# State-space set-up from turned tables: layouts, the W and T tables, and the order of the GLU's weight rows

## The chip, the cores and the metric

The kernel runs on one core of a Trainium2 chip. The metric is device time in microseconds (us) of one execution; the median of a few runs is compared. TensorE (PE in the profile) multiplies matrices, PEld is its weight load; VectorE (DVE), ScalarE (ACT) and GpSimd (POOL) do elementwise work; SyncE (SP) issues most DMAs, GpSimd's queue some.

## The reference

One inference step of a decoder with two layers, D_MODEL 1024, on a prompt of 512 tokens and 8 samples of 8 tokens: 576 tokens in all. Layer 0 mixes tokens by dilated attention, layer 1 by a diagonal complex state-space layer; each is followed by a gated ffn (D_FF 2816). The change concerns the state-space layer alone:

```python
def ssm_layer(h, state0, w_in, a_re, a_im, log_dt, b_re, b_im, c_re, c_im, d_skip, w_glu):
    u = h @ w_in                                     # 64 groups of 16 channels
    lam = complex(a_re, a_im); dt = exp(log_dt)[:, None]
    abar = exp(lam * dt)                             # (64 groups, 64 states)
    bbar = ((abar - 1) / lam)[..., None] * bmat      # (64, 64, 16)
    # x[t] = abar * x[t-1] + bbar u[t];   y[t] = Re(cmat x[t]) + d_skip * u[t]
    z = gelu(y) @ w_glu
    val, gate = split(z, 2)
    return val * sigmoid(gate), h_last
```

## The kernel before, in words

Activations lie with channels on the 128 partitions and the 576 tokens along the free dimension. A product in fp32 is made of three matmuls on halves hi and lo of both operands (`mm6`, L108). A weight tile of 512 KB is fetched into `raw` (4 buffers, SyncE's queue), ScalarE makes `whi` (L99), VectorE `wlo` (L100), and 48 matmuls use them: about 6.4 us.

In time the core goes through attention (0 to 400 us), the output projection `wo_phase` (to about 423), the ffn of layer 0 (`ffn`, to about 875), the state-space layer (`ssm_phase`, to about 1075) and the second ffn (`ffn_last`). Inside `ffn`, `tick()` is called behind each weight tile and takes one step of the generator `ssm_setup`. That generator makes the tables of the state-space layer while the ffn runs. A scheduler orders each engine's instructions from the program and its dependences; `issue_after` holds an instruction behind another one. SyncE's queue also carries copies of the attention caches (`o_kv_s`), of 1 MB each, a few per weight tile (`pace`).

The tables. Time is cut into 72 columns of 8 steps: an input tile U has 16 channels x 8 steps on the partitions and 72 columns per group. For each of eight blocks f (8 groups each) the set-up makes and writes to DRAM:

- W (`w_scr`): what 8 steps of input add to the state, B times powers of abar;
- V (`v_scr`): what a state gives to 8 steps of output, C times powers of abar;
- T (`t_scr`): the direct part of input on output within 8 steps, a block Toeplitz matrix of the kernel K, with D on its diagonal;
- E (`e_scr`): factors for the scan over columns, for all f at once.

Before: A, dt, C and the state are loaded as they lie and transposed on TensorE (L1386, L1440, L1453). Per f, `powers(f)` makes B times powers on VectorE (`wr`, L1329 to L1334); TensorE transposes it in 8 pieces (L1531) and ScalarE evicts it as W. K is 16 matmuls of `cb` (C in blocks) by `wr` (L1540), copied, transposed once more (L1548), spread by 8 stream shuffles (L1557), and multiplied by a mask (`tmask`, L1562) into T. GpSimd makes V. Two buffers `cb` are cleared at the start of the loop (L1506).

In `ssm_phase`, `stage1` makes u = W_in x, writes it to DRAM (`u_scr`, L1632) and reads it back with 8 steps on the partitions as `U` (L1636). `stage2` makes the states from U and W (L1646), a scan on VectorE follows; `stage3` makes y from U with T and from the states with V (L1687), gelu on ScalarE (L1689), and goes through DRAM again (`y_scr`, L1690, L1692) to the GLU. W, E, T and V of f = 4 to 7 are loaded on GpSimd's queue when buffers come free (L1293 to L1303).

Of the kernel before, what the change touches and what calls it, by code (L numbers as in the profile page):

```python
# [8 lines left out]
F32 = mybir.dt.float32  # L9
# [41 lines left out]
def _build(nc, tc, A, es):  # L51
# [108 lines left out]
    def acc(i=None):  # L160
        if i is None:
# [6 lines left out]
           "T": scr.tile([8, 128, 8, 128], F32, name="t_scr"), "E": scr.tile([8, 128, 2, 4, 64], F32, name="e_scr"), "U": scr.tile([8, 128, NT], F32, name="u_scr"),  # L168
# [1107 lines left out]
def ssm_setup(nc, tc, A, L, keep, out):  # L1276
    v, s, g, te = nc.vector, nc.scalar, nc.gpsimd, nc.tensor
    ident, pool, aux, scn = L["ident"], L["pool"], L["aux"], L["scn"]
    GP = 4096
# [18 lines left out]
    def consts_out(f, q):  # L1298
        kc = kp[f // 2 % 2]
        Tc = kc.tile([128, 8, 128], F32, name="Tc")  # L1300
        q.dma_start(Tc, scn["T"][f])
# [7 lines left out]

    out.update(Ar=Ar, Ai=Ai, E63=E63, rho=rho, x0=x0, xs0=xs0, KC=KC, consts_in=consts_in, consts_out=consts_out)  # L1310
    with ExitStack() as es:
        ct = es.enter_context(pool("ssa"))
        tmask = ct.tile([128, 8], F32, name="tmask")
        with tc.issue_after(L["xload"].ins):
            nc.sync.dma_start(tmask, A["c_tm"])
        dcol = ct.tile([128, KT], F32, name="dcol")
        with tc.issue_after(L["xload"].ins):
            nc.sync.dma_start(dcol, dram(A["ssm_d"], 0, [[1, 128], [128, KT]]))
        U8 = ct.tile([128, 2, 7, 32], F32, name="U8")
        dmask = ct.tile([128, 16], F32, name="dmask")  # L1320
        with tc.issue_after(L["xload"].ins):
            nc.sync.dma_start(dmask, A["c_dm"])
        Br = ct.tile([128, 32, 16], F32, name="Br")
        Bi = ct.tile([128, 32, 16], F32, name="Bi")
        Cr = ct.tile([128, 32, 16], F32, name="Cr")
        Cn = ct.tile([128, 32, 16], F32, name="Cn")
# [9 lines left out]
        with ExitStack() as e2:  # L1336
# [25 lines left out]
            raw = wk.tile([32, 3, 128], F32, name="raw")  # L1362
            with tc.issue_after(L["xload"].ins):
                nc.sync.dma_start(raw[:, 0], dram(A["ssm_a_re"], 0, [[128, 32], [1, 128]]))
            with tc.issue_after(L["xload"].ins):
                nc.sync.dma_start(raw[:, 1], dram(A["ssm_a_im"], 0, [[128, 32], [1, 128]]))
            ldt = wk.tile([32, 2], F32, name="ldt")
            with tc.issue_after(L["xload"].ins):
                nc.sync.dma_start(ldt, dram(A["ssm_log_dt"], 0, [[2, 32], [1, 2]]))
            with tc.issue_after(L["womark"].ins):  # L1370
                v.tensor_copy(raw[:, 2].rearrange("p (a b) -> p a b", a=2), ldt[:, :, None].to_broadcast([32, 2, 64]))
            cw = wk.tile([128, 2, 8, 64], F32, name="cw")
            with tc.issue_after(L["xload"].ins):
                nc.sync.dma_start(cw[:, 0], dram(A["ssm_c_re"], 0, [[64, 128], [8192, 8], [1, 64]]))
            with tc.issue_after(L["xload"].ins):
                nc.sync.dma_start(cw[:, 1], dram(A["ssm_c_im"], 0, [[64, 128], [8192, 8], [1, 64]]))
            bw = wk.tile([128, 2, 32, 16], F32, name="bw")
            with tc.issue_after(L["xload"].ins):
                nc.sync.dma_start(bw[:, 0], dram(A["ssm_b_re"], 0, [[16, 128], [2048, 32], [1, 16]]))
            with tc.issue_after(L["xload"].ins):  # L1380
                nc.sync.dma_start(bw[:, 1], dram(A["ssm_b_im"], 0, [[16, 128], [2048, 32], [1, 16]]))
            yield
            yield
            ps = aux.tile([128, 2, 512], F32, name="aux")
            for i in range(3):
                te.transpose(ps[:, 0, i * 32:(i + 1) * 32], raw[:, i], ident[:32, :32])  # L1386
            pc = wk.tile([128, 3, 32], F32, name="pc")
            v.tensor_copy(pc, ps[:, 0, :96].rearrange("p (a b) -> p a b", a=3))
# [14 lines left out]
            vexp(fl(mag), fl(lr), fl(n[:, :4]), fl(z[:, :4]), fl(sn[:, :4]), fl(ie))  # L1403
            th, n, z, sn, cn = (fl(x) for x in (th, n, z, sn, cn))
# [6 lines left out]
            v.scalar_tensor_tensor(sn, sn, 1.0, th, op0=OP.add, op1=OP.mult)  # L1411
            horner(cn, z, [(-1.0) ** k / math.factorial(2 * k) for k in range(8, 0, -1)])
# [4 lines left out]
            v.tensor_scalar(z, z, -2.0, 1.0, op0=OP.mult, op1=OP.add)  # L1417
            ui, ur = (x.rearrange("p (a b) -> p a b", b=32) for x in (th, z))
# [5 lines left out]
            t1, t2 = wk.tile([128, 4, 32], F32, name="t1"), wk.tile([128, 4, 32], F32, name="t2")  # L1424
            for m, n_ in ((2, 1), (4, 3)):
                w = slice(m + 1, m + 1 + n_)
                bc = lambda x: x[:, m:m + 1].to_broadcast([128, n_, 32])
                cmul(v, Ar[:, w], Ai[:, w], Ar[:, 1:1 + n_], Ai[:, 1:1 + n_], bc(Ar), bc(Ai), t1[:, :n_], t2[:, :n_])
# [3 lines left out]
            yield  # L1432
            yield
            for i, dst in ((0, Cr), (1, Cn)):
                ps = aux.tile([128, 2, 512], F32, name="aux")
                for f in range(8):
                    cwd = wk.tile([128, 2, 64], F32, name="cwd")
                    with tc.issue_after(L["womark"].ins):
                        v.tensor_copy(cwd, cw[:, i, f][:, None, :].to_broadcast([128, 2, 64]))
                    te.transpose(ps[:, f // 4, (f % 4) * 128:(f % 4 + 1) * 128], cwd.rearrange("p a b -> p (a b)"), ident)  # L1440
                for gl in range(2):
                    hs = slice(gl * 64, gl * 64 + 64)
                    for hf in range(2):
                        v.tensor_scalar(dst[hs, hf * 16:hf * 16 + 16, :], ps[hs, hf, :].rearrange("p (q l c) -> p q l c", l=2, c=16)[:, :, gl, :], 1.0 if i == 0 else -1.0, None, op0=OP.mult)
                yield
                yield
            yield
            xw = wk.tile([128, 2, 128, 2], F32, name="cw")
            nc.sync.dma_start(xw, dram(A["state_ssm"], 0, [[256, 128], [32768, 2], [1, 256]]))
            for hf in range(2):  # L1450
                for ri in range(2):
                    ps = aux.tile([128, 2, 512], F32, name="aux")
                    te.transpose(ps[:, 0, :128], xw[:, hf, :, ri], ident)  # L1453
                    v.tensor_copy(x0[:, ri, hf * 4:hf * 4 + 4, :], ps[:, 0, :128].rearrange("p (b q) -> p b q", b=4))
            for ri in range(2):
                for gl in range(2):
                    g.tensor_copy(xs0[ri * 64:ri * 64 + 64, gl], x0[gl * 64:gl * 64 + 64, ri])
# [17 lines left out]
            b12 = wk.tile([128, 2, 32, 16], F32, name="cw")  # L1475
            b1, b2 = b12[:, 0], b12[:, 1]
            bc = lambda x: x[:, :, None].to_broadcast([128, 32, 16])
            cmul(v, Br, Bi, bw[:, 0], bw[:, 1], bc(fr), bc(fi), b1, b2)
            yield
            yield  # L1480
# [21 lines left out]
        with ExitStack() as e2:  # L1502
            wk = e2.enter_context(pool("ssd", bufs=1))
            cb = [wk.tile([128, 4, 2, 16], F32, name=f"cb{i}") for i in range(2)]
            for t in cb:
                v.memset(t, 0.0)  # L1506
            sh = [128, 4, 16, 8]
            wr = {}

            def powers(f):  # L1510
                qs = slice(f * 4, f * 4 + 4)
                bw_ = lambda x: x[:, qs, :, None].to_broadcast(sh)
                rv = lambda x: x[:, 0:8, qs][:, ::-1, :].rearrange("p m q -> p q m")[:, :, None, :].to_broadcast(sh)
                wr[f] = wk.tile([128, 2, 4, 16, 8], F32, name="wr")
                wt = wk.tile([128, 2, 4, 16, 8], F32, name="wt")
                cmul(v, wr[f][:, 0], wr[f][:, 1], bw_(Br), bw_(Bi), rv(Ar), rv(Ai), wt[:, 0], wt[:, 1])
                for i, c in ((0, Cr), (1, Cn)):
                    for gl in range(2):
                        hs = slice(gl * 64, gl * 64 + 64)
                        v.tensor_copy(cb[i][hs, :, gl, :], c[hs, qs, :])  # L1520

            powers(0)
            yield
            yield
            for f in range(8):
                qs = slice(f * 4, f * 4 + 4)
                ps = aux.tile([128, 2, 512], F32, name="aux")
                with tc.issue_after(L["pem"][0].ins):
                    for ri in range(2):
                        for q in range(4):  # L1530
                            te.transpose(ps[:, ri, q * 128:(q + 1) * 128], wr[f][:, ri, q].rearrange("p c s -> p (c s)"), ident)  # L1531
                wo = wk.tile([128, 2, 4, 128], F32, name="wo")
# [354 lines left out]
```

## Time and profile before

| what | value |
|---|---|
| median of 3 runs | 1469.41 us (1469.1 to 1472.06) |
| profiled execution, its own time | 1472.93 us |
| its span | 1471.1 us |
| TensorE busy | 1432.1 us, 97% |
| VectorE, ScalarE, GpSimd busy | 1000.9, 596.0, 334.6 us |
| mean granted TensorE clock | 0.994 |
| moved by DMA | 345.73 MB |

The page gives busy time by engine and by group of instructions (line of the kernel, engine, operation, output <- inputs, count, busy us, mean ns, idle time before it and what ended it). The views of waits list for each engine which event it stood idle for; the timelines list single instructions with their start and length, idle time before them in brackets. In a window's row come its length, then busy us of each engine with the count of instructions, the granted clock, the DMA share and GB/s.

### The profile page before, as it was taken

How to read it: one execution, taken by the hardware profiler on the slowest of the kernel's cores; microseconds unless marked ns; L12 is line 12 of the kernel's file. 1: busy time of each engine (PE TensorE's matmuls, PEld its weight loads, DVE VectorE, ACT ScalarE, POOL GpSimd, SP SyncE). 2: the span in 40 equal slices, each digit the busy share in tenths (PEclk: the TensorE clock that was granted, in tenths of full speed). 3: DMA queues.
4: the chain of work that ended last, by engine and by line, in shares of the span. 5: the costliest groups of instructions: out<-in, count | busy, mean ns of one | idle time of the engine just before them, and what ended most of it. 6: DMA issues, size and time to landing. Idle time of an engine off the chain costs nothing. (4 is left out here: it accounts for less than half of the span.)

```text
span 1471.1 us, 30038 instructions
## 1 busy us (share of the span) xinstructions
PE 1432.1 (97%) x12398; PEld 1341.1 (91%) x12398; DVE 1000.9 (68%) x1696; ACT 596.0 (41%) x962; POOL 334.6 (23%) x410
## 2 busy tenths in 40 slices
PE   9999999999999999999999999699999999999998
PEld 7888777777899999999999999699999999999998
DVE  5898989745578653687777567856587646755772
ACT  4534455465462221223123363434365324532541
POOL 2022131320031066156245330131010001100110
PEclk9999999999999999999999999899999999999999
DMA  7566798999897757888979857964267767775532
GB/s 243 207 232 234 224 306 278 347 307 330 301 298 257 264 216 270 300 298 313 318 269 319 290 178 227 275 181 130 86 169 190 242 216 184 184 244 156 146 110 63
DMA packets 181048, 345.73 MB, mean 235 GB/s; under 512 B 40720, under 2 KB 116304, under 8 KB 179504
## 3 DMA queue, kind: packets, MB, share of 16 engines
q1 hardware_dynamic: 168176, 309.00, 61.4%
q0 software_dynamic: 9968, 32.12, 9.8%
q10 hardware_dynamic: 2768, 2.70, 0.6%
q8 instruction: 97, 1.59, 0.4%
q14 instruction: 39, 0.32, 0.1%
HBM read 312.29 MB, written 118.78 MB: 293 GB/s over the span
## 5 line engine op out<-in xcount | busy, mean ns | idle before, releaser
L108 PE MATMUL acc<-xgh,wlo 128*128 128x288 f32 x1056 | 227.6, 297 | 3.4 <-DVE wlo L100 3.4
L108 PE MATMUL acc<-xgh,whi 128*128 128x288 f32 x1056 | 229.5, 299 | 0.0
L108 PE MATMUL acc<-xgl,whi 128*128 128x288 f32 x1056 | 227.3, 297 | 0.0
L99 ACT ACTIVATE whi<-raw 128x1024 fp32r<-128x1024 f32 x98 | 102.0, 1041 | 242.8 <-PE acc L108 193.9
L1171 PE MATMUL bank<-xoh,whi 128*128 128x288 f32 x616 | 182.5, 296 | 4.2 <-ACT cq L1182 2.8
L1171 PE MATMUL bank<-xoh,wlo 128*128 128x288 f32 x616 | 181.7, 295 | 0.2 <-DVE wlo L1113 0.2
L1171 PE MATMUL bank<-xol,whi 128*128 128x288 f32 x616 | 181.7, 295 | 0.0
L108 PEld LDWEIGHTS acc<-xgh,wlo 128*128 128x128 f32 x1056 | 170.6, 189 | 4.0 <-DVE wlo L100 3.9
L108 PEld LDWEIGHTS acc<-xgh,whi 128*128 128x128 f32 x1056 | 170.3, 189 | 1.8 <-issue 1.2
L108 PEld LDWEIGHTS acc<-xgl,whi 128*128 128x128 f32 x1056 | 170.5, 189 | 0.1
L100 DVE TENSOR_TENSOR wlo<-raw,whi 128x1024 fp32r<-128x1024 f32 x98 | 124.7, 1272 | 67.3 <-ACT whi L99 66.3
L1171 PEld LDWEIGHTS bank<-xoh,whi 128*128 128x128 f32 x616 | 115.7, 188 | 6.1 <-ACT cq L1182 4.4
L1113 DVE TENSOR_TENSOR wlo<-raw,whi 128x1024 fp32r<-128x1024 f32 (+1 forms) x57 | 70.7, 1241 | 73.3 <-ACT whi L1112 73.3
L384 PE MATMUL acc<-whi,xh 128*128 128x512 f32 x288 | 118.7, 414 | 1.6 <-ACT xh L324 1.5
L1171 PEld LDWEIGHTS bank<-xoh,wlo 128*128 128x128 f32 x616 | 115.8, 188 | 0.6 <-DVE wlo L1113 0.6
L1171 PEld LDWEIGHTS bank<-xol,whi 128*128 128x128 f32 x616 | 115.7, 188 | 0.1
L1112 ACT ACTIVATE whi<-raw 128x1024 fp32r<-128x1024 f32 (+1 forms) x57 | 58.4, 1029 | 136.6 <-DMA raw<-ffn_w_down 52.1
L384 PE MATMUL acc<-wlo,xh 128*128 128x512 f32 x288 | 112.2, 391 | 0.0
L384 PE MATMUL acc<-whi,xl 128*128 128x512 f32 x288 | 111.5, 393 | 0.0
L108 PE MATMUL acc<-hh,whi 128*128 128x288 f32 x352 | 76.2, 297 | 0.0
L1080 POOL TENSOR_TENSOR gt<-gt,rstd 128x576 f32<-128x576 f32 x22 | 39.4, 1794 | 160.5 <-ACT gt L1079 160.4
L1127 POOL DMA_DIRECT2D s<-w_gu x22 | 19.4, 883 | 247.3 <-DMA s<-w_gu 145.5
(445 smaller groups left out, 3142.5 us busy)
## 6 DMA issues: line engine op xcount, KB each, us to landing
o_kv_s<-cache_kv_w SPq DMA_DIRECT2D x64, 1020.0 KB, 7.7
kc<-cache_kv_w SPq DMA_DIRECT2D x100, 512.0 KB, 6.9
raw<-ffn_w_down SPq DMA_DIRECT2D x40, 512.0 KB, 3.8
raw<-w_qkv SPq DMA_DIRECT2D x36, 512.0 KB, 7.0
raw<-w_gu SPq DMA_DIRECT2D x33, 512.0 KB, 3.4
kc<-qscr SPq DMA_DIRECT2D x32, 512.0 KB, 6.1
o_kv_s<-cache_kv_w SPq DMA_DIRECT2D x16, 1008.0 KB, 7.5
raw<-ffn_w_gate SPq DMA_DIRECT2D x22, 512.0 KB, 5.1
```

Source lines behind the costliest of these rows:

```text
L99: s.activation(hi, raw, AF.Copy)
L100: mark[0] = v.tensor_tensor(lo, raw, hi.bitcast(F32), OP.subtract)
L108: pem[0] = te.matmul(ps[:, c, :HN], w, x[:, c * HN:(c + 1) * HN], start=first and i == 0, stop=last and i == 2)
L384: ins = nc.tensor.matmul(*a, **kw)
L1080: g.tensor_tensor(t, t, nin.r, OP.mult)
L1112: s.activation(hi, raw, AF.Copy)
L1113: v.tensor_tensor(lo, raw, hi.bitcast(F32), OP.subtract)
L1127: g.dma_start(fl(t), block(c, m, k), accum_op=OP.add)
L1171: tc.keep_in_program_order(te.matmul(acc[q][:, :HN], a[:, k, i * 128:(i + 1) * 128], nin.x[x, k][b], skip_group_check=n != "a12", start=n ...
```

## The change

All small inputs of the state-space layer are laid out on the host as the core wants them (`_ssm`: A and dt, B in two layouts, C, the state, D), and each is loaded without a transpose. The rows of `ssm_w_glu` are reordered to channel within step of the output tile. In the set-up, A times the factor of B is made for all f at once (`af`), transposed by 4 matmuls and written to DRAM (`a_scr`); per f it is read back with its rows repeated 16 times, B with its rows repeated 8 times (`bt`), and VectorE's products of the two are W with channels on the partitions. K is now 16 matmuls of B (`Bz`) by table V (`vx`, 9 powers, made on GpSimd); it is copied into `kk`, 15 blocks of which 7 are zero, and one DMA writes T's 8 overlapping views of it. u is stored with time reversed; y is written in whole rows and read back in pieces of 72 columns. The chain that makes the exponentials no longer waits for a mark behind `wo_phase`, and takes more steps of the generator.

```diff
-    cb = [wk.tile([128, 4, 2, 16], F32, name=f"cb{i}") for i in range(2)]
-    for t in cb:
-        v.memset(t, 0.0)
...
+            def load(f):
+                a = wk.tile([128, 2, 4, 128], F32, name="af")
+                nc.sync.dma_start(a..., dram(scn["A"], f * 8192, [[0, 16], [1024, 8], [1, 1024]]))
+                b = wk.tile([128, 2, 4, 128], F32, name="bt")
+                nc.sync.dma_start(b..., dram(A["s_bt"], f * 16384, [[1024, 16], [0, 8], [1, 1024]]))
+                c = wk.tile([128, 2, 4, 16], F32, name="C", bufs=2)
+                nc.sync.dma_start(c, A["s_c"][:, :, f * 4:f * 4 + 4])
...
-                            te.transpose(ps[:, ri, q * 128:(q + 1) * 128], wr[f][:, ri, q]..., ident)
-                s.activation(wo.rearrange("p r q c -> p r (q c)"), ps, AF.Copy)
-                nc.sync.dma_start(scn["W"][f], wo)
+                for h in range(2):
+                    v.tensor_tensor(t, x, b2(1), OP.mult)
+                    v.tensor_tensor(x, x, b2(0), OP.mult)
+                    v.tensor_tensor(x[:, 0], x[:, 0], t[:, 1], OP.subtract)
+                    v.tensor_tensor(x[:, 1], x[:, 1], t[:, 0], OP.add)
+                    if h:
+                        nc.sync.dma_start(scn["W"][f], a)
...
-                            te.matmul(pk[q * 32:q * 32 + 32, 0, :128], cb[i][:, q]..., wr[f][:, i, q]..., ...)
-                v.tensor_copy(kk, pk[:, 0, :128])
-                    te.transpose(pk[:, 1, :128], kk, ident)
-                    v.stream_shuffle(st[:, t], kt, m)
-                v.tensor_tensor(tt..., st, tmask[:, :, None].to_broadcast([128, 8, 128]), OP.mult)
-                nc.sync.dma_start(scn["T"][f], tt.rearrange("p g c t -> p g (c t)"))
+                            te.matmul(pk[q * 32:q * 32 + 32, 0, :128], Bz[:, i, f * 4 + q]..., vx[:, i, q, 0:8]..., ...)
+                v.scalar_tensor_tensor(k[:, 7], dmask, dcol[:, f:f + 1], pk[:, 0, :16], op0=OP.mult, op1=OP.add)
+                v.tensor_copy(k[:, 8:15], pk[:, 0, 16:128].rearrange("p (t c) -> p t c", c=16))
+                nc.sync.dma_start(scn["T"][f].rearrange("g (c s) x -> (g c) s x", s=8), bass.AP(tensor=k0.tensor, offset=k0.offset, ap=[list(k0.ap[0]), [16, 8], [1, 128]]))
...
-        q.dma_start(Tc, scn["T"][f])
+        q.dma_start(Tc, scn["T"][f].rearrange("g p c -> p g c"))
...
-            v.tensor_tensor(u, ps[m][:, :, :HN], nin.r, OP.mult)
+            v.tensor_tensor(pos(u)[:, ::-1, ::-1, :], pos(ps[m][:, :, :HN]), pos(nin.r), OP.mult)
...
-        nc.sync.dma_start(dram(scn["Y"], f * 128 * NT, [[72, 128], [9216, 8], [1, 72]]), ys...)
+        nc.sync.dma_start(scn["Y"][f], ys.rearrange("p q l c -> p (q l c)"))
-        nc.sync.dma_start(yt, scn["Y"][f])
+        nc.sync.dma_start(yt, dram(scn["Y"], f * 128 * NT, [[72, 128], [9216, 8], [1, 72]]))
```

Three places in the order of instructions. First VectorE at the first norm of the ffn (`rs_m`, `sq`, `rstd`) and its first use (`gt`), before:

```order
L1371 COPY raw<-ldt 32x128
L1439 COPY cwd<-cw 128x128
L100 TENSOR_TENSOR wlo<-raw,whi 128x1024
L181 SCALAR_TENSOR_TENSOR xgl<-xT,gm,xgh 128x576
L100 TENSOR_TENSOR wlo<-raw,whi 128x1024
L212 TENSOR_SCALAR rs_m<-aux 128x288 x2
L214 TENSOR_TENSOR sq<-rstd 128x576
L215 TENSOR_TENSOR sq<-sq,rs_m 128x576
L221 SCALAR_TENSOR_TENSOR rstd<-sq,rstd 128x576
L1078 TENSOR_TENSOR gt<-acc_5403,rstd 128x576
```

and after, where the chain of the exponentials (`z`, `th`, `n`, `mag`) stands among them:

```order
L212 TENSOR_SCALAR rs_m<-aux 128x288
L1386 SCALAR_TENSOR_TENSOR th<-n,th 128x320
L1340 SCALAR_TENSOR_TENSOR z<-z,sn 128x128
L1387 TENSOR_SCALAR th<-th 128x320
L214 TENSOR_TENSOR sq<-rstd 128x576
L1353 TENSOR_SCALAR z<-z 128x128
L215 TENSOR_TENSOR sq<-sq,rs_m 128x576
L1355 TENSOR_TENSOR mag<-z,ie 128x128
L221 SCALAR_TENSOR_TENSOR rstd<-sq,rstd 128x576
L1388 TENSOR_TENSOR z<-th 128x320
L1411 COPY rho<-mag 128x32
L1078 TENSOR_TENSOR gt<-acc_5404,rstd 128x576
```

The chain, which stood behind this norm, now stands ahead of it and between its steps. Second, VectorE at the start of the loop over f, before:

```order
L1506 MEMSET cb_7279 128x128
L1506 MEMSET cb_7280 128x128
L1329 TENSOR_TENSOR wt<-Br,Ar 128x512
L1330 TENSOR_TENSOR wt<-Bi,Ai 128x512
L1520 COPY cb_7279<-Cr 64x4x16 x2
L1520 COPY cb_7280<-Cn 64x4x16 x2
L1331 TENSOR_TENSOR wr<-wt 128x512
L1332 TENSOR_TENSOR wt<-Br,Ai 128x512
L1333 TENSOR_TENSOR wt<-Bi,Ar 128x512
L1334 TENSOR_TENSOR wr<-wt 128x512
L100 TENSOR_TENSOR wlo<-raw,whi 128x1024
```

and the products of W that open it now, from `af` (A's powers, repeated) and `bt` (B, repeated):

```order
L1513 TENSOR_TENSOR wt<-af,bt 128x512
L1514 TENSOR_TENSOR af<-af,bt 128x2x256
L1515 TENSOR_TENSOR af<-af,wt 128x256
L1516 TENSOR_TENSOR af<-af,wt 128x256
L1513 TENSOR_TENSOR wt<-af,bt 128x512
L1514 TENSOR_TENSOR af<-af,bt 128x2x256
L1515 TENSOR_TENSOR af<-af,wt 128x256
L1516 TENSOR_TENSOR af<-af,wt 128x256
L100 TENSOR_TENSOR wlo<-raw,whi 128x1024
```

The clearing of `cb` and the powers are gone from VectorE; products of what two DMAs loaded stand first. Third, SyncE in the state-space layer, where u of the last two blocks (f = 6, 7) goes out and comes back, before:

```order
L87 DMA raw<-ssm_w_glu 128x4x256 x2
L1690 DMA y_scr<-ys 128x8x72
L1632 DMA u_scr<-yt 128x576
L1692 DMA U<-y_scr 128x576
L1632 DMA u_scr<-yt 128x576
L87 DMA raw<-ssm_w_glu 128x4x256
L1636 DMA U<-u_scr 128x8x72
L1690 DMA y_scr<-ys 128x8x72
```

and after:

```order
L87 DMA raw<-ssm_w_glu 128x4x256 x2
L1649 DMA y_scr<-ys 128x576
L1651 DMA U<-y_scr 128x8x72
L1591 DMA u_scr<-yt 128x576 x2
L87 DMA raw<-ssm_w_glu 128x4x256
L1595 DMA U<-u_scr 128x8x72
L1649 DMA y_scr<-ys 128x576
```

The read of y(0), which waits for the write of y(0), moved ahead of both writes of u; these now follow each other.

More of the change, by code (lines that the diff above doesn't have):

```diff
@@ L1360, in vexp @@
                 v.tensor_tensor(y, q, ie.bitcast(F32), OP.mult)
[L1362 to L1376, printed above, removed]
-            bw = wk.tile([128, 2, 32, 16], F32, name="bw")
[L1378 to L1381, printed above, removed]
+            pc = wk.tile([128, 3, 32], F32, name="pc")
+            early(pc, A["s_a"])
+            bw = wk.tile([128, 2, 32, 16], F32, name="bw")
+            early(bw, A["s_b"])
+            early(x0, A["s_x"])
+            for ri in range(2):
+                early(xs0[ri * 64:ri * 64 + 64], dram(A["s_x"], ri * 256, [[512, 64], [64 * 512, 2], [1, 256]]))
+            g.memset(Bz, 0.0)
             yield
             yield
[L1384 to L1388, printed above, removed]
             ar, ai = pc[:, 0], pc[:, 1]
@@ L1427, in ssm_setup @@
                 bc = lambda x: x[:, m:m + 1].to_broadcast([128, n_, 32])
-                cmul(v, Ar[:, w], Ai[:, w], Ar[:, 1:1 + n_], Ai[:, 1:1 + n_], bc(Ar), bc(Ai), t1[:, :n_], t2[:, :n_])
+                f1, f2 = (two[:, i, :n_ * 32].rearrange("p (m q) -> p m q", q=32) for i in range(2))
+                cmul(v, Ar[:, w], Ai[:, w], Ar[:, 1:1 + n_], Ai[:, 1:1 + n_], bc(Ar), bc(Ai), f1, f2)
             v.tensor_copy(rho, mag[:, 3])
@@ L1431, in ssm_setup @@
             v.tensor_copy(U8[:, 1], ui[:, 3:10])
[L1432 to L1457, printed above, removed]
             yield
@@ L1579, in ssm_setup @@
+            yield
         consts(0, nc.sync)
```

154 lines of the change are left out of this document (80 added, 74 removed).

## The prediction

> **What bounds the kernel now.** I read the page's busy times first, then TensorE's waits, then its groups of the set-up, then the timelines at the places where those rows lie.
>
> ```profile
> PE 1432.1 (97%) x12398; PEld 1341.1 (91%) x12398; DVE 1000.9 (68%) x1696; ACT 596.0 (41%) x962; POOL 334.6 (23%) x410
> ```
>
> ```profile
> PE acc L1646 <- DMA U<-u_scr: 11.6, 2, 10.9
> PE acc L108 <- DVE wlo L100: 3.4, 2, 2.5
> ```
>
> TensorE is busy for 1432.1 of 1471.1 us. So an edit pays in two ways only: it takes matmuls out of TensorE's stream, or it shortens one of the few waits. The two largest waits both lie in code that the change touches: 10.9 us in the state-space stage (L1646) and 2.5 us behind VectorE in the ffn (L108). VectorE and ScalarE work saved elsewhere is worth nothing by itself.
>
> **Part 1: transposes leave TensorE.** The set-up runs as a filler between the ffn's weight tiles of 48 matmuls. Its TensorE groups, and ScalarE's start on successive weight tiles (first a stretch without set-up matmuls, then one whole turn of the loop over f):
>
> ```profile
> L1531 PE MATMUL aux<-ident,wr 128*128 128x128 f32 x64 | 8.3, 272 | 0.0
> L1540 PE MATMUL aux<-wr,cb 128*32 128x128 f32 x128 | 5.2, 279 | 0.0
> L1440 PE MATMUL aux<-ident,cwd 128*128 128x128 f32 x16 | 4.3, 271 | 0.0
> L1548 PE MATMUL aux<-ident,kk 128*128 128x128 f32 x8 | 2.2, 271 | 0.0
> ```
>
> ```profile
> 540.95 1.06 ACT L99 ACTIVATE whi<-raw 128x1024 fp32r<-128x1024 f32 x1 [5.29 <-PE acc L108]
> 547.35 1.06 ACT L99 ACTIVATE whi<-raw 128x1024 fp32r<-128x1024 f32 x1 [5.34 <-PE acc L108]
> ...
> 643.55 1.06 ACT L99 ACTIVATE whi<-raw 128x1024 fp32r<-128x1024 f32 x1 [4.13 <-issue]
> 650.72 1.05 ACT L99 ACTIVATE whi<-raw 128x1024 fp32r<-128x1024 f32 x1
> 657.22 1.06 ACT L99 ACTIVATE whi<-raw 128x1024 fp32r<-128x1024 f32 x1 [1.70 <-PE acc L108]
> 663.62 1.06 ACT L99 ACTIVATE whi<-raw 128x1024 fp32r<-128x1024 f32 x1 [1.18 <-DMA o_kv_s<-cache_kv_w]
> 670.88 1.06 ACT L99 ACTIVATE whi<-raw 128x1024 fp32r<-128x1024 f32 x1 [1.90 <-PE acc L108]
> ```
>
> The 271 ns of one transpose is its length in the pipeline, not its price. The price is what a tile takes above 6.40 us (547.35 − 540.95). The four tiles of one f take 7.17, 6.50, 6.40 and 7.26 us. The first holds the 16 kernel matmuls (L1540, +0.77), which stay. The second holds the kk transpose (L1548, +0.10) and the fourth the 8 W transposes (L1531, +0.86): 0.96 us per f, 7.7 us over 8. The 16 C transposes (L1440) and, by the diff, 4 of the state and 3 of A and dt are 23 more at the same 0.11 us: 2.5 us. Four new transposes of af cost 0.4. Net −9.8 us, and this is on the path, since TensorE has no idle time there. The kernel matmuls only exchange their operands, in the same shape: 0.
>
> **Part 2: the wait at the loop's start goes.** SyncE writes e_scr; VectorE's first memset of the loop reuses its memory and waits for the write, and the powers then stand ahead of the next weight split (L100), on which TensorE waits:
>
> ```profile
> 576.83 0.69 SPq L1499 DMA_DIRECT2D e_scr<-ee  x1
> 586.52 0.31 DVE L1506 MEMSET cb<- 128x128 f32 x2 [4.85 <-DMA e_scr<-ee]
> 594.07 1.22 DVE L100 TENSOR_TENSOR wlo<-raw,whi 128x1024 fp32r<-128x1024 f32 x1
> 595.35 0.53 PE L108 MATMUL acc<-xgh,wlo 128*128 128x288 f32 x2 [2.45 <-DVE wlo L100]
> ```
>
> ```profile
> 579.35 1.06 ACT L99 ACTIVATE whi<-raw 128x1024 fp32r<-128x1024 f32 x1 [5.34 <-PE acc L108]
> ...
> 608.98 1.06 ACT L99 ACTIVATE whi<-raw 128x1024 fp32r<-128x1024 f32 x1 [1.36 <-PE acc L108]
> ...
> 597.00:599.00 2.00, 2.00 (x10) 2.00 (x9) 1.59 (x3) 0.98 (x2) 0.21 (x1) 0.50 1.93 760
> ```
>
> These four tiles took 29.63 us instead of 25.60: 4.0 lost, 2.45 waiting and the rest at the granted clock of 0.50 that followed. After the change no VectorE instruction stands there on e_scr: the loads of af and GpSimd's memset of kk do. VectorE first needs af two tiles after its load is issued, 12.8 us against the 9.7 us (576.83 to 586.52) that the write took. So −4.0, with 0 as the other bound.
>
> The Trainium skill ("TensorE: Matmul & The Clock Gate", Part 1) has the half clock follow an idle window of about 3.4 us. Here a wait of 2.45 us was enough (0.50 above); by the page this stall would have cost 2.45 and not 4.0, and the sum would end 1.6 us higher; the trace decides.
>
> **Part 3: the loop over f.** VectorE loses the powers, 8 stream shuffles, the mask multiply and two copies out of PSUM per f, and gains eight products over 256 columns. All that lies beside TensorE, and VectorE is busy for 170.68 of 230 us as it is, so 0; ScalarE loses an eviction, 0; GpSimd's V table grows from 6 operations to 7, and nobody waits for it closely, 0. What grows is DMA: per f, af and bt 512 KB each and C 64 KB, 8.9 MB in all.
>
> ```profile
> 600.00:830.00 230.00, 230.00 (x1826) 227.08 (x1825) 170.68 (x311) 60.84 (x69) 105.65 (x61) 1.00 0.85 298
> ...
> raw<-ffn_w_gate SPq DMA_DIRECT2D x22, 512.0 KB, 5.1
> ```
>
> The DMA engines are 0.85 busy at 298 GB/s, that is 350 GB/s when busy; 8.9 MB is 25.4 us of the 34.5 us (15% of 230) that are idle. Covered, but nearly used up. The cover is the weight prefetch: four raw buffers are about 25 us ahead at 6.4 us a tile, while a tile lands in 5.1. I take +0.5 for small waits; the ends are 0 and +6 (rival C).
>
> **Part 4: VectorE at the start of the ffn.** The set-up's scalar chain no longer waits for a mark behind the w_o stage or for TensorE, so it enters VectorE's queue between the residual adds and the ffn's first norm.
>
> ```profile
> 400.00:425.00 25.00, 25.00 (x190) 25.00 (x189) 21.61 (x42) 13.81 (x20) 9.38 (x6) 1.00 0.99 275
> 425.00:450.00 25.00, 25.00 (x186) 24.58 (x185) 13.97 (x33) 11.72 (x15) 5.62 (x3) 1.00 0.99 353
> ...
> 429.58 1.13 PE L206 MATMUL aux<-ssum,ones 128*128 128x288 f32 x4
> 438.17 1.42 DVE L1078 TENSOR_TENSOR gt<-acc,rstd 128x576 f32<-128x576 f32 x2
> ...
> L1345 DVE SCALAR_TENSOR_TENSOR z<-z,sn 128x32 f32<-128x32 f32 x7 | 1.3, 190 | 0.2
> L1345 DVE SCALAR_TENSOR_TENSOR z<-z,sn 128x128 f32<-128x128 f32 x7 | 3.2, 461 | 0.0
> L1407 DVE SCALAR_TENSOR_TENSOR th<-n,th 128x320 f32<-128x320 f32 x3 | 1.4, 483 | 0.0
> ```
>
> About 13 us of small operations (some 35 of 32 columns at 0.17 to 0.19 us, a dozen of 128 columns, and half a dozen of 320, these rows the dear ones) fall where VectorE idles 3.4 and 11.0 us in the two windows. Much of that idle time is made of waits inside the residual and norm chains, so small operations will delay these. I estimate the last residual 4 us later, the norm's matmuls (L206) stalled about 1.5 us, and gt about 1.5 us too late for TensorE's next accumulator, of which part is the same delay: +2, between 0 and +6 (6 with a half-clock stretch as in part 2).
>
> **Part 5: the state-space stage.** The change writes u reversed and reads y back in another form, and lays T out so that one f's T is read in 1024 runs of 512 B, not 128 rows of 4 KB. SyncE's and GpSimd's queues around the 10.9 us wait, that wait, a window over it, and the landing times of the U reads (L1636) and of the y reads (L1692):
>
> ```profile
> 926.95 0.34 SPq L1632 DMA_DIRECT2D u_scr<-yt  x1
> 930.74 0.33 SPq L1692 DMA_DIRECT2D U<-y_scr  x1
> 931.19 1.27 SPq L1632 DMA_DIRECT2D u_scr<-yt  x1
> 932.50 0.44 SPq L87 DMA_DIRECT2D raw<-ssm_w_glu  x1
> 933.36 0.39 SPq L1636 DMA_DIRECT2D U<-u_scr  x1
> ...
> 929.38 0.53 POOL L1301 DMA_DIRECT2D Tc<-t_scr  x1 [2.29 <-PE acc L1687]
> ...
> 946.14 1.11 PE L1646 MATMUL acc<-U,Wc 128*64 128x72 f32 x14 [10.91 <-DMA U<-u_scr]
> ...
> 938.00:950.00 12.00, 3.86 (x64) 3.89 (x66) 6.97 (x14) 2.40 (x8) 0.00 (x0) 0.50 1.03 302
> ...
> DMA to landing us min/median/max: 3.1/4.6/12.6
> ...
> DMA to landing us min/median/max: 2.7/2.9/5.5
> ```
>
> The read U(6) is issued at 933.36 and lands after 12.6 us, where 4.6 is the median. GpSimd's three pairs of Tc and Vc (3 MB from 929.38 on) fill the engines: 12 us at 302 GB/s is 3.6 MB. SyncE's queue holds then, on each of 16 engines, about 96 small pieces (32 of 1 KB of w_glu, 64 of 288 B of U), GpSimd's 48 of 4 KB. If an engine takes one piece from either queue in turn, SyncE's 96 pieces outlast GpSimd's 48, and everything lands together: 243 KB per engine at 22 GB/s is 11 us, which fits 12.6. With T in 512 B pieces, 96 turns take 64 of 512 B, 8 of 4 KB and 24 of 512 B beside them: 127 KB, 5.8 us. The order also moves: U<-y_scr(0) now stands ahead of u_scr(6), which costs that write 0.5 to 1 us, while the second u_scr, the weight tile and U(6) follow about 2 us earlier. The bounds are −13 (the whole wait and the 2.2 us of half clock behind it) and +4 (the read of y, which waits for a write, blocks the queue). I take −6, an estimate nearer the first mechanism, as short pieces have some cost of their own. At the stage's end the y read in 288 B pieces adds 0.4 us (U reads, in such pieces, take 3.1 us at best; y reads, in rows so far, 2.7).
>
> The Trainium skill ("DMA: Bandwidth & Descriptors", Queues, rings and completion order) has an engine drain a whole packet, some 9 to 17 pieces, from a queue before it switches. By it the size of T's pieces would not decide, and the sum would keep most of the wait (rival A).
>
> **Sum.** −9.8 − 4.0 + 0.5 + 2.0 − 6.0 + 0.4 = −16.9 against the profiled execution's own 1472.93, that is 1456.0. The median of the runs, 1469.41, lies 3.5 below that execution, so 1452.5; I say 1453.
>
> **Rivals.**
> A. The U(6) wait stays, as the same bytes lie in the engines: −10.9, 1459. For it: the DMA share of 1.03 in that window. Against: U moves ahead in its queue. Chance 0.22.
> B. The wait grows by 4, the y read blocking SyncE ahead of u_scr(6): 1463. For it: that read was issued 3.8 us after the instruction ahead of it (926.95 to 930.74). Chance 0.10.
> C. Slower: DMA becomes the bound in the loop. The new loads and the short T pieces would have to cost over twice the 25.4 us that their bytes say: 34.5 are idle, and weights are about 19 us ahead (25 less a landing). From 53.5 us on TensorE starves; the gain is eaten up at 70 us (2.75 times), and at three times (76 us) 23 us are lost and the kernel ends at 1476. For it: the 0.85 share with many short pieces. Chance 0.05.
> D. Part 4's chain costs 6 or more, with half clock, and e_scr's wait only moves to the af loads (+4): 1461. Chance 0.13.
> My forecast, within about 5 us of 1453, has the remaining 0.50.
>
> **How the numbers follow.** The range 1443 to 1463 reaches from the whole U wait gone (−7 more) with a small part 4 (−2) to rivals A and D; about 0.2 is left out, B's upper half and C with it. A measurement here tells about 0.2%, 2.9 us, from no change: faster means below 1466.5. All of the forecast, of A and of D lie below, and 0.04 of B: 0.89. The rest of B, with a larger part 4, and C's milder half are within: 0.07. Slower is the rest of C: 0.04.
>
> **What would show it.** Tiles in the loop of 6.4 us but for one of 7.2 per f; no 0.50 window at 597; a VectorE wait at L206 or L1078 of 1 to 3 us; U(6) landing in 6 to 8 us and a TensorE wait on L1646 of 3 to 6 us; a DMA share near 0.95 in the loop with no weight wait above 1 us. I am wrong if TensorE's waits on raw, af or bt appear in the loop, or if the wait on L1646 stays above 10 us.

## The result: slower by about 0.8%, and the profile after

The changed kernel takes 1481.15 us (median of 5, 1480.14 to 1485.73) against 1470.94 (median of 5, 1469.1 to 1472.65; three of them are the runs behind the 1469.41 above) for the kernel before: a ratio of 1.0076, 95% interval 1.0057 to 1.0095, some 11 us slower. The profiled execution is the longest of the five, 1485.73 us with a span of 1483.9, 4.6 above the median; sums over its trace have to be read with that in mind.

Busy time and TensorE's waits of the changed kernel (line numbers have moved: L1605 is the U product that was L1646):

```profile
PE 1428.0 (96%) x12307; PEld 1335.4 (90%) x12307; DVE 958.2 (65%) x1512; ACT 588.8 (40%) x955; POOL 338.9 (23%) x416
...
PE acc L108 <- DVE wlo L100: 16.9, 6, 11.7
PE acc L1605 <- DMA U<-u_scr: 12.7, 1, 12.7
...
PE aux L206 <- POOL ssum L199: 1.3, 1, 1.3
```

TensorE has 91 matmuls fewer, the number that the prediction counted (95 transposes gone, 4 new), and VectorE is busy for 43 us less. But TensorE's wait behind VectorE, 3.4 us before, is 16.9, and its wait for U, which was to halve, grew from 11.6 to 12.7 in total, the longest from 10.9 to 12.7.

Where the time went is read from ScalarE's starts on weight tiles (L99), the clock of the whole stretch. The two profiled executions differ by 12.8 us in span. Of this, −2.5 lie ahead of the w_o stage and +2.1 behind the stretch around the wait for U, 2.0 of them behind the layer's last weight tile; the code there is the same, so I count both as differences between executions. The rest: +6.4 from the w_o stage to the 22nd tile; +4.0 in the set-up's loop; +0.1 up to the second half of the state-space stage; +2.7 there, in the stretch around the wait for U. The +4.0 is a large loss and two gains. The loss is one place:

```profile
570.41 1.06 ACT L99 ACTIVATE whi<-raw 128x1024 fp32r<-128x1024 f32 x1 [5.34 <-PE acc L108]
591.34 1.06 ACT L99 ACTIVATE whi<-raw 128x1024 fp32r<-128x1024 f32 x1 [19.87 <-PE acc L108]
...
657.36 1.06 ACT L99 ACTIVATE whi<-raw 128x1024 fp32r<-128x1024 f32 x1 [4.49 <-PE acc L108]
664.50 1.06 ACT L99 ACTIVATE whi<-raw 128x1024 fp32r<-128x1024 f32 x1 [1.43 <-PE acc L108]
670.90 1.06 ACT L99 ACTIVATE whi<-raw 128x1024 fp32r<-128x1024 f32 x1 [4.63 <-PE acc L108]
677.30 1.06 ACT L99 ACTIVATE whi<-raw 128x1024 fp32r<-128x1024 f32 x1 [1.30 <-PE acc L108]
683.70 1.06 ACT L99 ACTIVATE whi<-raw 128x1024 fp32r<-128x1024 f32 x1 [4.37 <-PE acc L108]
```

One tile at the loop's start took 20.93 us, 14.5 too long. The four tiles of an f take 7.14, 6.40, 6.40 and 6.40 us, 26.34 instead of 27.33: the transposes are gone at the price that was worked out. What happened in those 20.93 us, on SyncE (with its wait for e_scr, and the landing time of bt from the view of DMA, both for 545 to 575), VectorE, GpSimd and in windows:

```profile
549.50 0.68 SPq L1474 DMA_DIRECT2D e_scr<-ee  x1
558.21 0.57 SPq L1484 DMA_DIRECT2D af<-a_scr  x1
560.03 0.58 SPq L1486 DMA_DIRECT2D bt<-s_bt  x1
...
SPq L1484 <- DMA e_scr<-ee: 4.4, 1, 4.4
bt<-s_bt SPq DMA_DIRECT2D x1, 512.0 KB, 11.1
...
571.22 0.69 DVE L1513 TENSOR_TENSOR wt<-af,bt 128x512 f32<-128x512 f32 x1 [11.28 <-DMA Ec<-e_scr]
574.40 1.58 DVE L1513 TENSOR_TENSOR wt<-af,bt 128x512 f32<-128x512 f32 x1
580.41 2.41 DVE L100 TENSOR_TENSOR wlo<-raw,whi 128x1024 fp32r<-128x1024 f32 x1
...
571.41 0.74 POOL L1503 TENSOR_SCALAR C<-C 128x64 f32<-128x64 f32 x1 [12.96 <-DMA C<-s_c]
572.13 1.58 POOL L1505 TENSOR_TENSOR vx<-C,Ar 128x576 f32<-128x576 f32 x1
...
571.00:583.00 12.00, 0.29 (x3) 0.12 (x1) 11.61 (x10) 0.47 (x1) 11.36 (x9) 0.67 0.99 350
583.00:588.00 5.00, 5.00 (x21) 5.00 (x22) 2.29 (x3) 0.00 (x0) 0.91 (x1) 0.50 1.13 378
```

SyncE could issue the load of af only when e_scr had landed, 8.7 us after its issue; bt followed behind a weight tile and a copy of 1 MB. VectorE came to the first product at 559.94 (571.22 less 11.28) and stood there until 571.2. The row names Ec, which is no operand of the product; bt is one, and it landed 11.1 us after its issue at 560.03, that is at 571.1. The eight products then took 9.2 us, and only then came the weight split (580.41) on which TensorE had been waiting since 571. The window shows TensorE nearly empty for 12 us; 5 us at a clock of 0.50 followed.

In the w_o stage and the ffn's first tiles TensorE now stands still, and its clock falls:

```profile
400.00:425.00 25.00, 22.80 (x166) 21.93 (x166) 22.11 (x50) 10.78 (x15) 7.62 (x5) 1.00 0.76 285
425.00:450.00 25.00, 22.24 (x151) 21.47 (x150) 23.63 (x67) 13.60 (x16) 8.44 (x4) 0.93 0.57 197
...
405.90 1.41 DVE L1348 TENSOR_SCALAR sn<-pc 128x32 f32<-128x32 f32 x1 [1.88 <-DMA xr<-x_scr]
407.43 0.17 DVE L1343 TENSOR_SCALAR n<-sn 128x32 f32<-128x32 f32 x1
...
405.85 1.42 POOL L199 TENSOR_TENSOR ssum<-ssum,sq 128x576 f32<-128x576 f32 x1 [9.18 <-ACT sq L198]
```

VectorE is busy for 45.7 of 50 us there (35.6 before), TensorE idles 5.0. Two operations of the chain on 32 columns tell more: one took 1.41 us, the other 0.17. The long one ends together with GpSimd's addition L199 (405.85 + 1.42 = 407.27; VectorE goes on at 407.23). In the kernel before, the same operation took 0.18 us:

```profile
443.73 0.18 DVE L1353 TENSOR_SCALAR sn<-pc 128x32 f32<-128x32 f32 x1
```

In the state-space stage, SyncE's queue and the U product:

```profile
930.05 0.34 SPq L1649 DMA_DIRECT2D y_scr<-ys  x1
937.75 0.37 SPq L1651 DMA_DIRECT2D U<-y_scr  x1
938.17 1.10 SPq L1591 DMA_DIRECT2D u_scr<-yt  x2
939.32 0.77 SPq L87 DMA_DIRECT2D raw<-ssm_w_glu  x1
945.58 0.37 SPq L1595 DMA_DIRECT2D U<-u_scr  x1
...
955.83 2.19 PE L1605 MATMUL acc<-U,Wc 128*64 128x72 f32 x32 [12.65 <-DMA U<-u_scr]
```

The read of y(0) waited until 937.75 for its write, and the writes of u went behind it. Counted from the same weight tile (926.08 before, 934.05 now), the first of them, that of u(6), went 3.2 us later than before; the second stood behind that read before too. U(6) was issued 4.2 us later and landed after some 10 us, where 12.6 were seen before, so TensorE could start on it 1.7 us later.

### The profile page after: what moved, and what is told of

The parts are those of the page before. It is cut to its first block, busy times and chain, and to the rows that moved or that the text cites. A ratio compares the mean times of both kernels' runs of the same rounds, so it can differ in the third digit from the quotient of the medians.

```text
span 1483.9 us, 29688 instructions
## 1 busy us (share of the span) xinstructions
PE 1428.0 (96%) x12307; PEld 1335.4 (90%) x12307; DVE 958.2 (65%) x1512; ACT 588.8 (40%) x955; POOL 338.9 (23%) x416
## 5 line engine op out<-in xcount | busy, mean ns | idle before, releaser
L99 ACT ACTIVATE whi<-raw 128x1024 fp32r<-128x1024 f32 x98 | 102.0, 1041 | 265.5 <-PE acc L108 237.8
L100 DVE TENSOR_TENSOR wlo<-raw,whi 128x1024 fp32r<-128x1024 f32 x98 | 130.2, 1329 | 102.5 <-ACT whi L99 100.6
L108 PE MATMUL acc<-hh,wlo 128*128 128x288 f32 x352 | 76.8, 300 | 11.7 <-DVE wlo L100 11.7
```

Source lines behind the costliest of these rows:

```text
L99: s.activation(hi, raw, AF.Copy)
L100: mark[0] = v.tensor_tensor(lo, raw, hi.bitcast(F32), OP.subtract)
L108: pem[0] = te.matmul(ps[:, c, :HN], w, x[:, c * HN:(c + 1) * HN], start=first and i == 0, stop=last and i == 2)
```

## Experiments

Each was timed on one chip together with the kernel before, whose median there was 1471.7 to 1472.6 us; ratios are to that, and 0.1% is 1.47 us. For the state-space stage the table gives the stretch between two starts of ScalarE on weight tiles around the wait for U (926.08 to 973.85 in the kernel before). The last two columns come from one trace each. How far such a value can be trusted is shown by kernels whose code of this stage is the same: the changed kernel, e1 and e2 have stretches of 49.5 to 50.5 us, e3 and e4 waits of 5.6 and 10.6 us. So a difference of 1 us in the stretch tells nothing, nor do 5 us in the wait.

| kernel | median us | ratio, 95% interval | TensorE's longest wait on U, us | stretch, us |
|---|---|---|---|---|
| before | 1470.94 | 1 | 10.9 | 47.8 |
| changed | 1481.15 | 1.0076, 1.0057 to 1.0095 | 12.7 | 50.5 |
| e1 products later | 1471.68 | 1.0007, 0.9989 to 1.0025 | 12.0 | 49.5 |
| e2 chain behind norm | 1477.01 | 1.0035, 1.0020 to 1.0051 | 12.8 | 50.3 |
| e3 read of y(0) late | 1482.40 | 1.0069, 1.0041 to 1.0097 | 5.6 | 49.4 |
| e4 all three | 1465.72 | 0.9950, 0.9927 to 0.9973 | 10.6 | 49.7 |
| e5 before, T in 512 B | 1474.57 | 1.0021, 0.9997 to 1.0044 | 12.1 | 49.2 |
| e6 T, V loads cut | 1475.64 | 1.0040, 1.0022 to 1.0058 | 0.4 | 41.9 |
| e7 cut, y(0) late | 1478.63 | 1.0060, 1.0041 to 1.0079 | 0.5 | 44.1 |
| e8 five edits | 1461.91 | 0.9935, 0.9917 to 0.9952 | 1.0 | 46.4 |
| e9 e8, y(0) as changed | 1463.97 | 0.9942, 0.9920 to 0.9964 | 3.3 | 50.4 |
| e10 four products later | 1462.68 | 0.9933, 0.9912 to 0.9954 | 3.0 | 50.5 |
| e11 gate alone | 1482.98 | 1.0082, 1.0054 to 1.0110 | 3.4 | 50.1 |

**e1: the first products of W later.**

```diff
             ab = load(0)
             yield
+            yield
...
+                    with ExitStack() as hold:
+                        if f + h == 0:
+                            hold.enter_context(tc.issue_after(L["mark"][0].ins))   # the last weight split
-                    v.tensor_tensor(t, x, b2(1), OP.mult)
+                        v.tensor_tensor(t, x, b2(1), OP.mult)
```

> The changed kernel, but VectorE's first products of W stand behind a later weight split, some five weight tiles later; the loads of af, bt and C stay where they are. Theory: TensorE lost 14.5 us at the loop's start only because VectorE, which runs in order, stood 11.3 us at these products until bt had landed, with a weight split behind them. Then the wait of 11.7 us goes, four tiles there take 25.6 us, and the kernel takes about 1467 us. Rival: the products themselves are slow (9.2 us for eight, beside GpSimd's V table) and delay the split wherever they stand; then 4 to 5 us stay and it takes about 1472. Second rival: the DMA engines are full, and the wait comes back as waits for raw, af or bt: 1478 or more.

The ratio fell by 0.69%, 10 us. The median, 1471.68, is near the first rival's figure, but its cause is not there. The place itself is healed completely, 6.40 us where 20.93 stood, and from the 22nd tile to the end of the loop this trace has 281.2 us, the changed kernel's 297.0:

```profile
576.10 1.07 ACT L99 ACTIVATE whi<-raw 128x1024 fp32r<-128x1024 f32 x1 [5.34 <-PE acc L108]
582.50 1.06 ACT L99 ACTIVATE whi<-raw 128x1024 fp32r<-128x1024 f32 x1 [5.33 <-PE acc L108]
```

The loads stayed where they were: bt is issued 10.5 us behind e_scr in both kernels (562.63 less 552.12 in e1). So the cause is shown: the place of the products in VectorE's order, not DMA capacity and not the products' own time. That 10 and not 14.5 us came back in the median fits the profiled execution of the changed kernel being 4.6 us above its median; the tile took 19.94, 17.81, 16.15 and 18.00 us in the traces of e3, e6, e7 and e11, which leave this place as it is, a stall of 9.8 to 13.5 us (in e2, where two tiles share it, 12.9).

**e2: the chain of the exponentials behind the norm.**

```diff
+            yield
+            pc0, pc = pc, wk.tile([128, 3, 32], F32, name="pch")
+            with tc.issue_after(L["mark"][0].ins):
+                v.tensor_copy(pc, pc0)
             ar, ai = pc[:, 0], pc[:, 1]
```

> The changed kernel, but the chain of the exponentials starts from a copy of its inputs that VectorE makes behind the first gt, so that no operation of the chain stands among the last residuals and the ffn's first norm. Theory: the chain there cost TensorE about 9 us (5.0 idle, the rest half clock and late residuals): about 1472 us, and TensorE is busy for 25.0 of 25 us in both windows from 400 to 450. Rival: the same work of VectorE only moves behind the norm and delays gt, ut and the splits of the first ffn tiles: 3 us gained at most, 1478.

The ratio fell by 0.41%, 6 us. TensorE's idle time in the two windows is gone:

```profile
400.00:425.00 25.00, 25.00 (x189) 25.00 (x189) 21.75 (x40) 13.97 (x20) 9.42 (x6) 1.00 1.05 379
425.00:450.00 25.00, 25.00 (x187) 24.79 (x186) 16.99 (x50) 10.87 (x13) 5.39 (x3) 1.00 0.54 194
```

From the w_o stage to the 22nd tile the trace has 134.2 us, the changed kernel 141.3, the kernel before 135.0. The chain's place cost 7.1 us in the traces and 6 in the times; the theory's 9 was too much, and its 1472 us was missed by 5. The rival is refuted: the same work behind the norm delays nothing that TensorE waits for.

**e3: the read of y(0) behind the reads of u.** In `stage3(0)` the read is kept back and issued in `stage1(3)` behind the last read of U:

```diff
-        nc.sync.dma_start(yt, dram(scn["Y"], f * 128 * NT, [[72, 128], [9216, 8], [1, 72]]))
+        rd = lambda yt=yt, f=f: nc.sync.dma_start(yt, dram(scn["Y"], f * 128 * NT, ...))
+        if f == 0:
+            late.append(rd)
...
+        while c == 3 and late:
+            with tc.issue_after(ul.ins):        # ul: the last read of U
+                late.pop()()
```

> The changed kernel, but the read of y(0) stands behind the last read of u on SyncE's queue. Theory: that read, waiting for the write of y(0), held both writes of u for 7.7 us; without it U(6) is issued 3 to 5 us earlier and TensorE's wait on L1605 falls from 12.7 to 8 or 9 us: about 1477 us. Rival: the engines are full until GpSimd's T and V loads are through, so U(6) lands when these land, whenever it is issued: wait above 11 us, 1480 to 1481.

Both expectations failed in part. SyncE issued U(6) 5.1 us behind the weight tile, where the changed kernel has 11.5, and TensorE's longest wait for U fell, more than foreseen; ScalarE's `ys` waited for a write of y:

```profile
PE acc L1608 <- DMA U<-u_scr: 7.4, 3, 5.6
...
PE aux L1649 <- ACT ys L1651: 2.3, 1, 2.3
...
ACT ys L1651 <- DMA y_scr<-ys: 13.1, 1, 13.1
```

But the time did not fall: neither the stretch (49.4) nor the run differs from the changed kernel's by more than such values scatter. Part of what was saved on U came back as waits for `ys`, whose buffers the writes of y hold. The order on SyncE's queue alone did not shorten this stage.

**e4: all three together.**

> All three edits together (products later, chain behind the norm, read of y(0) behind U). Theory: the three losses add up, 14.5 + 9 + 4 us, and leave what the prediction had counted on, about 1454 us, 16 us faster than the kernel before. Rival: parts of them are one loss seen twice, or DMA becomes the bound when the waits go: 1462 us or more.

The ratio is 0.9950, 1.26% below the changed kernel; the three edits alone gave 0.69, 0.41 and 0.07, together 1.17%. The gains add up, and the kernel with the three edits is faster than the one before. 1454 was not reached: U's wait is still 10.6 us although U(6) was issued 5.7 us behind the weight tile, much as in e3 and with the same code of the stage (why e3 has 5.6 is open), and the loop has a new loss of about 4 us at f = 1, where VectorE waited 10 us for af. There is one buffer for af: W(0) is written from it, and the next load goes behind that write.

**e5: the kernel before, with T in pieces of 512 B.**

```diff
...
-        q.dma_start(Tc, scn["T"][f])
+        q.dma_start(Tc, scn["T"][f].rearrange("g p c -> p g c"))
...
-                nc.sync.dma_start(scn["T"][f], tt.rearrange("p g c t -> p g (c t)"))
+                nc.sync.dma_start(scn["T"][f].rearrange("g p c -> p g c"), tt.rearrange("p g c t -> p g (c t)"))
```

> The kernel before, with T stored by group, so that its writes and its loads are 1024 runs of 512 B each and not 128 rows of 4 KB; nothing else changed. Theory of the prediction: an engine takes one piece from each queue in turn, so that short T pieces let U(6) through: TensorE's longest wait on L1646 falls from 10.9 to about 5 us and the kernel takes about 1465 us. Rival: the bytes in the engines decide, not the number of pieces: the wait stays between 9 and 13 us and the time within 0.2% of before.

```profile
PE acc L1646 <- DMA U<-u_scr: 12.7, 2, 12.1
```

The wait did not fall from 10.9 to about 5 but stood at 12.1, and the time did not fall. What the prediction drew from its picture of one piece from each queue in turn is refuted for this size of pieces. By the Trainium skill ("DMA: Bandwidth & Descriptors", Queues, rings and completion order) an engine drains packets of several pieces from a queue before it switches. By that rule the size of T's pieces would not decide, and the run agrees with that much; it does not show the packets themselves.

**e6 and e7: the loads of T and V cut to an eighth** for f = 4 to 6, in the changed kernel and in e3. The rest of these tiles is zero, so these two kernels leave out most of y of three blocks:

```diff
-        q.dma_start(Tc, scn["T"][f].rearrange("g p c -> p g c"))
+        n = 1 if 4 <= f < 7 else 8
+        if n == 1:
+            q.memset(Tc, 0.0)
+        q.dma_start(Tc[:, :n], scn["T"][f, :n].rearrange("g p c -> p g c"))      # V likewise
```

> The changed kernel with the loads of T and V for f = 4, 5 and 6 cut to an eighth (the rest of these tiles is zero, so y of these blocks isn't the reference's). Theory: the 3 MB on GpSimd's queue are what the writes of u and the read of U(6) wait beside in the engines; without them u_scr and U(6) land in 4 to 5 us each and the wait on L1605 falls from 12.7 to 4 us or less: about 1472 us. Rival: the order on SyncE's queue, the read of y(0) ahead of the writes of u, makes the wait by itself: then 9 us or more stay, 1479.

> The kernel with the read of y(0) behind U, and with the same loads of T and V cut to an eighth (y of f = 4 to 6 isn't the reference's). Theory: both causes gone, the wait for U(6) is below 1.5 us, no other wait of TensorE takes its place in the stage, and the kernel takes about 1469 us. Rival: the chain of y (gelu, write, read) is the stage's real bound, as with the read of y(0) moved alone; then the waits on U go but TensorE waits for ys and for the GLU's inputs instead, and the time is that of the cut loads alone, within 2 us.

With the loads cut, the wait for U vanished with the read of y(0) still ahead of the writes of u, and the stretch fell by 8.6 us, the ratio by 0.36% (5 us, where 9 were expected). The read of y(0) then held nothing up: it was issued 0.5 us behind the weight tile, against 3.7 in the changed kernel. So what GpSimd loads beside U makes the wait. The other traces agree: with all loads in place, U(6) was issued 5.7 (e4), 7.3 (before), 10.2 (e1), 11.5 (changed) and 11.9 us (e2) behind the weight tile, and TensorE could go on at 19.9, 20.1, 21.1, 21.8 and 22.0. Six us of earlier issue bring two; only e3's trace, with 5.1 and 14.7, stands apart. In e6 these are 5.9 and 9.5. e7 was no better, its stretch 2.3 us longer: TensorE waits there 4.2 us for `ys` (0.3 in e6), so the late read of y(0) delays the chain of y, as its rival had it. The times of e6 and e7 can't be told apart.

**e8 to e11: can T and V simply come later?** e8 adds to e4 that the products of f = 1 stand behind a later split, and a gate on GpSimd's queue. e9 is e8 without e3's edit, e10 is e9 with `f < 4` for `f < 2`, e11 is the changed kernel with the gate alone.

```diff
+                for _ in range(1 if f == 1 else 0):
+                    yield
...
-                        if f + h == 0:
+                        if f < 2 and h == 0:
...
+        if f == 1:
+            gate.append(g.tensor_copy(kp.tile([128, 1], F32, name="gate"), Uc[6][:, 0, :1]))
         if f < 4:
+            with ExitStack() as hold:
+                if gate:
+                    hold.enter_context(tc.issue_after(gate[0].ins))
-            consts_out(f + 4, g)
+                consts_out(f + 4, g)
```

> All three edits of before (products later, chain behind the norm, read of y(0) behind U), and two more: the products of f = 1 also stand behind a later weight split, since SyncE's write of W(0) and the next load of af are one after the other in one buffer and VectorE waited 10 us for them; and GpSimd loads T and V of f = 5 and later only behind a copy that reads U(6). Theory: the loop has no tile above 7.2 us but for one or two, the wait for U(6) falls from 10.6 to 3 us, and the kernel takes 1455 to 1457 us. Rival: T and V then come late, TensorE waits for them at f = 5 as long as it did for U(6), and the kernel takes 1462.

> The kernel of the run e8, but with the read of y(0) where the changed kernel has it, ahead of the last writes of u. Theory: with T and V of f = 5 to 7 held back, U(6) lands soon in either order, and moving the read of y(0) only delays gelu and the y chain: the stretch from f = 4's GLU weights to the next split (37.8 us in e8) falls to 34 to 36 us, the kernel to 1459 or 1460 us. Rival: the read of y(0) still holds the writes of u by 4 us or more, and the stretch is as long as in e8 or longer: 1462 to 1465.

> As e9, but the products of f = 0 to 3, not of 0 and 1 alone, stand behind a later weight split. Theory: the wait that e8 had at f = 2 (about 2 us, behind the load of af) is gone, and nothing else is: 1 to 2 us less than e9. Rival: the wait moves on to f = 4: the same as e9.

> The changed kernel with one edit: GpSimd loads T and V of f = 5, 6 and 7 only behind a copy that reads U(6). Theory: what GpSimd loads beside the writes and reads of u is what makes the wait of 12.7 us; it falls to 5 us or less, and the kernel takes 1474 to 1477 us, as with the loads cut. Rival: T and V are then late and the stage waits for them: no gain, 1480 to 1482.

The gate alone (e11) took the wait for U from 12.7 to 3.4 us and gained nothing:

```profile
PE acc L1605 <- DMA U<-u_scr: 4.5, 2, 3.4
PE acc L108 <- ACT ys L1648: 4.4, 1, 4.4
...
PE acc L1646 <- DMA Vc<-v_scr: 1.1, 1, 1.1
```

The time moved to `ys` and V, as the rival said. The same shows in e9 (stretch 50.4). Only together with the late read of y(0), in e8, did the stretch shrink, to 46.4 in its one trace, with no wait for U(6) left (the 1.0 us in the table is for an earlier U, as are e7's 0.5). That e9's stretch would be shorter than e8's was wrong; the times of the two runs can't be told apart. e10 removed the loop's stall at f = 2 in the trace (tiles of 7.16 and 6.40 us where e8 and e9 had 12.02 and 2.99), but its time can't be told from theirs. e8 and e10 have the lowest ratios, 0.65 and 0.67% below the kernel before; e8 does not reach the 1455 to 1457 that was expected.

## Why the prediction was wrong, by its own steps

- **Part 1 (−9.8) held.** 26.34 us for the four tiles of an f against 27.33: 7.9 us over eight f, where 7.7 were foreseen. The early transposes' 2.5 us can't be separated in the changed kernel; e2, which has them out and the chain behind the norm, is 0.7 us shorter there than the kernel before.
- **Part 2 (−4.0) failed, and it is the step that decides.** VectorE's wait for e_scr did go: the four tiles that took 29.63 us take 25.64, at the full clock (1.00 in the windows 597 to 599 and 600 to 830). But "VectorE first needs af two tiles after its load is issued" counted tiles in the order of two queues, as if a load were issued where it stands. It stood behind a wait for that very write of e_scr (issue at 558.21, 8.7 us behind e_scr's own), bt behind two more transfers, so that it landed at 571.1, and a VectorE with nothing else to do arrived at 559.94. The wait was handed from one instruction to another and grew, because now 8 products stood between it and the next weight split: a loss of 10 to 14 us in the traces, 10 in time by e1, where a gain of 0 was the worst end given. In the prediction's terms, the landing of bt and the eight products ahead of the split were put at nothing. Rival D names af's load, but prices it at 4.
- **Part 3 (+0.5) held roughly.** One pair of tiles lost 1.2 us; with a DMA share of 0.96 from 600 to 830, as high as foreseen, TensorE waited for no weight. Rival C did not occur.
- **Part 4 (+2, at most 6) was too small.** 7.1 us in the traces, 6 by e2. The mechanism was right: VectorE's chain delays what TensorE waits for (5.0 us of idle TensorE and a clock of 0.93 in the second window), and the 1.3 us at L206 are the 1.5 foreseen there. The size was not: waits of 1.0, 0.7, 0.4 and 1.4 us behind weight splits and an operation of the chain were not in the estimate. One reason is likely, though no run takes it alone: the operations' lengths came from a stretch where GpSimd had little to do (the chain's old place), and here four of them took 1.3 to 1.4 us instead of about 0.2, each beside GpSimd's L199.
- **Part 5 (−6.0 and +0.4) had the wrong sign: +2.7.** The term from T's smaller pieces is refuted by e5. The reordered read of y(0) (rival B) did put the write of u(6) 3.2 us later, and U(6), which was to be issued 2 us earlier, was issued 4.2 later; yet e3 and e11 show that with that order or the loads' timing changed alone, TensorE waits for `ys`, T or V in place of U, so that neither is the price by itself. What GpSimd loads beside U is, as e6 shows: without most of it 8.6 us go. But the kernel before has these loads too. Why the stretch grew by 2.7 rather than stayed is not settled: the y read in short pieces, T in short runs and the order all differ, e5 (T's runs alone) is 1.4 above the kernel before, and 1 us lies within the scatter.

The sum, from the traces: +6.4 in the w_o stage and the ffn's first tiles (with the early transposes gone), +4.0 in the loop (14.5 − 4.0 − 7.7 + 1.2), +2.8 behind it, together 13.2 us. With the loop's stall at the 9.8 to 13.5 us of the other traces it is 8.5 to 12.2; measured are 11. That the first two are the main part is shown by e1, e2 and e4: out one by one they give 10 and 6 us back, and with both out (and the read of y(0) moved, which alone gave nothing that can be told) the kernel is 0.5% faster than before.

The forecast of 1453 was missed by 28 us. Part 2 accounts for 10 to 14 of them, part 5 for 8 and part 4 for 5; without part 2's step alone (e1) the kernel would have been as fast as before, not faster. One of the two signs of being wrong that the prediction named came true, the wait at the U product above 10 us. The other, waits of TensorE on raw, af or bt, came in another form: VectorE waited for bt, and TensorE for VectorE.

## What to carry to other kernels

Where a change takes away a wait, ask what the freed engine reaches next and when that is ready: an engine that waits at one instruction holds everything that stands behind it in its order, here the one split that TensorE needed. Time a load from the moment its queue can issue it, with the waits ahead of it and a landing time under the load of that moment, not from its place in the order. And when a wait for one transfer is due to the bytes beside it, moving transfers about can just move the wait: here it went only with fewer bytes (e6), or with slack made on both sides (e8).

## What the runs showed of the hardware

A short VectorE operation can take as long as a GpSimd operation beside it: `sn<-pc` on 32 columns took 1.41 us, ending with GpSimd's L199, and 0.18 us in the kernel before, where no GpSimd operation ran beside it. The product L1513 took 1.58 us when GpSimd's V table was already running, and 0.68 us for the next f, with GpSimd quiet; its mean over the loop is 1.0:

```profile
599.98 0.68 DVE L1513 TENSOR_TENSOR wt<-af,bt 128x512 f32<-128x512 f32 x1
...
L1513 DVE TENSOR_TENSOR wt<-af,bt 128x512 f32<-128x512 f32 x16 | 16.2, 1012 | 13.7 <-DMA Ec<-e_scr 11.3 <-DMA af<-a_scr 2.2
```

The Trainium skill ("SBUF — State Buffer", Who interferes with whom) says that VectorE shares a pair of ports with GpSimd. In its two-port modes the one that issues first has the pair for the whole instruction and the other is blocked; with two inputs in SBUF VectorE contends with a GpSimd instruction that reads SBUF. The lengths agree with both; no run here shows the ports themselves.
